# RMSNorm with every row written twice: the first load of each group in two transfers of 512 rows, gamma in two DMAs

## The chip, the cores and the metric

The kernel runs on one core of one Trainium2 chip. The metric is the device time of one launch in microseconds (us); lower is better. The time before is the median of three runs, 238.38 us (238.24 to 238.87). A profile is one more execution of the same program, recorded by the hardware profiler: its own time was 238.07 us, of which 236.2 us lie between the first and the last instruction of the core (the span). All times of the trace count from the start of that span.

The core's engines run their own instruction streams side by side: ACT (the scalar engine), DVE (the vector engine), POOL and SP. SP does no arithmetic here; it issues the DMAs of x and of the output. A DMA runs on 16 DMA engines, which cut it into packets.

## The reference

```python
def reference(x, gamma):          # x: (8, 512, 2048) float32, gamma: (2048,) float32
    B, S, D = x.shape
    x_rep = np.repeat(x, 2, axis=1)
    rms = np.sqrt((x_rep ** 2).mean(axis=-1, keepdims=True) + 1e-6)
    x_norm = x_rep / rms
    return (x_norm * gamma[None, None, :]).astype(np.float32)
```

Each of the 4096 rows of x (2048 floats, 8 KB) is divided by its root mean square, multiplied by gamma, and written twice, one copy right behind the other. So 33.55 MB are read and 67.11 MB written.

## The kernel before

**Tiles.** The rows are taken in four blocks of 1024 (index n). In a block, partition p holds eight neighbouring rows (H * K = 8), 64 KB of x in one piece: `x_t` at line 36 is the view. One DMA loads a block (8.39 MB). Its output has 2048 rows and is stored in two DMAs (h = 0, 1) of 8.39 MB each: for h, partition p writes the doubled copies of its rows 4h to 4h + 3, 64 KB in one piece, so neighbouring partitions lie 128 KB apart in the output (`out_t`, line 37). There are twelve such transfers in all, four loads and eight stores.

**Memory.** One buffer `y` (line 46) has 24 slots of one row (8 KB) a partition. `first` is slots 0 to 7, `second` 8 to 15, `third` 16 to 23; each is the size of one store. A group of two blocks is worked through by `four(n, ...)` (line 89), which is called for n = 0 and n = 2:

- block n is loaded into slots 4 to 11, that is the upper half of `first` and the lower half of `second`;
- block n + 1 is loaded into `third`;
- rows 0 to 3 of block n (slots 4 to 7) are scaled into the even slots of `first`, copied into the odd ones, and stored (h = 0);
- rows 4 to 7 of block n (slots 8 to 11) are scaled within `second`, from the last row to the first, copied and stored (h = 1);
- rows 0 to 3 of block n + 1 go from `third` into `first`, which has to wait until the first store has read `first`; then rows 4 to 7 are spread within `third`. Both are copied and stored.

**Instructions.** `squares` (line 57) takes the sum of squares of one row a partition on ACT (line 63) and then the root of all rows of the call (line 67). `scale` (line 70) has a reciprocal on DVE (line 73) and one multiplication by the row's factor and by gamma (line 75). `repeat` (line 80) makes the second copies, on ACT or on DVE (line 82).

**Order.** The schedule is written by hand: each engine works its instructions in the order in which the program lists them, and the framework adds the waits that the slots need. On SP the order in a group is load n, load n + 1, then the four stores; SP waits at each one until its slots may be read or written, and what stands behind it waits too. In the second group the load of block 2 (slots 4 to 11) has to wait for the second and the third store of the first group, the load of block 3 for the fourth.

**Gamma.** `constants` (line 121) loads gamma on ACT's queue into partition 0 of `y`, as a staging place: 16 pieces of 125 floats in one DMA (line 122), and three DMAs of 16 floats (line 128). POOL then spreads it over all partitions into `gamma_b` in two broadcasts (lines 132 and 136). The same function sets the epsilon and has ACT load its table with a first root (line 140).

Of the kernel before, what the change touches and what calls it, by code (L numbers as in the profile page):

```python
# [1 line left out]

# [4 lines left out]


@with_exitstack
def kernel(  # L10
    ctx: ExitStack,
    tc: tile.TileContext,
    x: bass.AP,
    gamma: bass.AP,
    out: bass.AP,
):
    nc = tc.nc
    P = nc.NUM_PARTITIONS
    f32 = mybir.dt.float32
    Act = mybir.ActivationFunctionType  # L20
    Alu = mybir.AluOpType

    B, S, D = x.shape
    Bo, So, Do = out.shape
    R = So // S
    assert R == 2 and D == Do and B == Bo and So == S * R
    eps = 1e-6
    inv_d = 1.0 / float(D)


    K = 4
    N = B * S
    ntiles = N // (P * K)
    assert N % (P * K) == 0 and ntiles == 8
    H = 2
    x_t = x.rearrange("b s d -> (b s) d").rearrange("(n p k) d -> n p k d", p=P, k=H * K)
    out_t = out.rearrange("b s d -> (b s) d").rearrange("(n p h j) d -> n h p (j d)", p=P, h=H, j=K * R)

    singles = ctx.enter_context(tc.tile_pool(name="singles", bufs=1))
    rows = ctx.enter_context(tc.tile_pool(name="rows", bufs=1))  # L40
    junk = ctx.enter_context(tc.tile_pool(name="junk", bufs=1, space=bass.MemoryType.PSUM))
    small = ctx.enter_context(tc.tile_pool(name="small", bufs=4))

    y = rows.tile([P, 3 * K * R, D], f32, name="y")
    first, second, third = 0, K * R, 2 * K * R

    def load(n, at):
        nc.sync.dma_start(out=y[:, at : at + H * K, :], in_=x_t[n])  # L50

    def store(n, h, to):
        nc.sync.dma_start(
            out=out_t[n, h], in_=y[:, to : to + K * R, :].rearrange("p j d -> p (j d)")
        )

    def squares(at, rows):

        n = len(rows)
        ss = small.tile([P, n], f32, name=f"ss{n}")  # L60
        for c, k in enumerate(rows):
            sq = junk.tile([P, D], f32, name="sq")
            nc.scalar.activation(  # L63
                out=sq[:], in_=y[:, at + k, :], func=Act.Square, accum_out=ss[:, c : c + 1]
            )
        rms = small.tile([P, n], f32, name=f"rms{n}")
        nc.scalar.activation(out=rms[:], in_=ss[:], func=Act.Sqrt, scale=inv_d, bias=eps_t[:])  # L67
        return rms

    def scale(at, to, rows, rms):  # L70
        n = len(rows)
        rstd = small.tile([P, n], f32, name=f"rstd{n}")
        nc.vector.reciprocal(out=rstd[:], in_=rms[:])  # L73
        for c, k in enumerate(rows):
            nc.vector.scalar_tensor_tensor(  # L75
                out=y[:, to + R * k, :], in0=y[:, at + k, :], scalar=rstd[:, c : c + 1],
                in1=gamma_b[:], op0=Alu.mult, op1=Alu.mult,
            )

    def repeat(to, k0, k1, copy):  # L80
        y_r = y[:, to + R * k0 : to + R * k1, :].rearrange("p (k r) d -> p k r d", r=R)
        copy(out=y_r[:, :, 1, :], in_=y_r[:, :, 0, :])  # L82

    ctx.enter_context(tc.manual_schedule())

    half = K // 2
    up, down = list(range(K)), list(range(K - 1, -1, -1))

    def four(n, constants, step):


        load(n, first + K)
        constants()
        load(n + 1, third)
        for rows in (up[:half], up[half:]):
            scale(first + K, first, rows, squares(first + K, rows))
        repeat(first, 0, half, nc.scalar.copy)
        repeat(first, half, K, nc.vector.tensor_copy)
        store(n, 0, first)
        scale(second, second, down, squares(second, down))  # L100
        repeat(second, half, K, nc.scalar.copy)
        for k in range(0, half, step):
            repeat(second, k, k + step, nc.vector.tensor_copy)
        store(n, 1, second)
        roots = [squares(third + h * K, up) for h in range(H)]
        scale(third, first, up, roots[0])
        repeat(first, 0, half, nc.scalar.copy)
        repeat(first, half, K, nc.scalar.copy)
        store(n + 1, 0, first)
        scale(third + K, third, up, roots[1])  # L110
        repeat(third, 0, K, nc.scalar.copy)
        store(n + 1, 1, third)

    gamma_b = singles.tile([P, D], f32, name="gamma_b")
    G, E = 16, 3
    C = D // G - E
    gamma_s = y[0:1, 0:2, :].rearrange("p k (c d) -> p (k c) d", c=G // 2)
    gamma_t = y[0:1, 2, :]
    eps_t = singles.tile([P, 1], f32, name="eps_t")

    def constants():
        nc.scalar.dma_start(
            out=gamma_s[0:1, :, :C],
            in_=gamma[: G * C].rearrange("(p c d) -> p c d", p=1, c=G),
        )
        for c in range(E):
            at = G * C + c * G
            nc.scalar.dma_start(
                out=gamma_t[0:1, c * G : (c + 1) * G],
                in_=gamma[at : at + G].partition_broadcast(1),  # L130
            )
        nc.gpsimd.partition_broadcast(  # L132
            out_ap=gamma_b[:, : G * C].rearrange("p (c d) -> p c d", c=G),
            in_ap=gamma_s[0:1, :, :C],
        )
        nc.gpsimd.partition_broadcast(out_ap=gamma_b[:, G * C :], in_ap=gamma_t[0:1, : E * G])  # L136
        nc.vector.memset(eps_t, eps)  # L137

        root = singles.tile([P, 1], f32, name="root")[:]
        nc.scalar.activation(out=root, in_=eps_t[:], func=Act.Sqrt)  # L140

    four(0, constants, half)
    four(2, lambda: None, 1)


# [1 line left out]
_INS = ['x', 'gamma']  # L147
_OUTS = [((8, 1024, 2048), 'float32')]


# [23 lines left out]
```

## Time and profile before

| what | value |
|---|---|
| median of three runs | 238.38 us (238.24 to 238.87) |
| time of the profiled execution | 238.07 us |
| its span | 236.2 us |
| L75 DVE, scaling of one row, x32 | 73.8 us, 2349 ns each |
| L63 ACT, squares of one row, x32 | 60.1 us, 1878 ns each |
| L82 ACT, copies, x10 | 42.6 us, 4283 ns each |
| L82 DVE, copies, x5 | 9.2 us, 1865 ns each |
| L132 and L136 POOL, broadcasts of gamma | 2243 and 323 ns |
| ACT's idle time before L63, ended by the load of x | 70.4 us, twice |

How to read it: a line number is that of the printed kernel. "Busy" is the sum of the durations of a group of instructions; the idle time before a group is put down to what ended it. The share of a DMA queue is the time that its packets took, out of the span of all 16 DMA engines. A release by a DMA is the moment when the transfer's last part has landed.

### The profile page before, as it was taken

Reading aid. Unit: us, or ns where it says so; the run is one execution under the profiler, and the core shown is the slowest. Engines: PE = TensorE matmul, PEld = TensorE weight load, DVE = VectorE, ACT = ScalarE, POOL = GpSimd, SP = SyncE. Lnnn points to the kernel's source line nnn. Section 1 sums busy time; section 2 is a strip of 40 time slices with the busy share of each in tenths; the row PEclk is TensorE's granted clock in tenths of the full one; section 3 lists DMA queues with packets and bytes.
Section 4 is the critical chain, followed back from the end, with each engine's and each line's share of the span. In section 5 each row is a group of like instructions: output and inputs, shape, how many; then the busy total and the mean of one; then the engine's idle time right before and its main releaser. Section 6 shows DMA issues by size and latency. Waiting matters only on the chain.

```text
span 236.2 us, 226 instructions
## 1 busy us (share of the span) xinstructions
DVE 84.5 (36%) x48; ACT 110.2 (47%) x86; POOL 2.8 (1%) x6
## 2 busy tenths in 40 slices
DVE  0000396594699500000000007928919992000000
ACT  2001989479998470000000049991999957400000
POOL 0110000000000000000000000000000000000000
DMA  9898989989898989989898998989898998989894
GB/s 355 356 533 355 510 377 422 466 366 522 355 533 356 533 355 422 466 377 510 355 533 355 488 400 355 533 355 533 355 533 355 488 399 355 533 355 533 355 533 178
DMA packets 1767, 100.68 MB, mean 426 GB/s; under 512 B 230, under 2 KB 230, under 8 KB 230
## 3 DMA queue, kind: packets, MB, share of 16 engines
q1 hardware_dynamic: 1728, 100.66, 98.7%
q10 hardware_dynamic: 38, 0.01, 0.0%
q14 instruction: 1, 0.01, 0.0%
HBM read 33.56 MB, written 67.11 MB: 426 GB/s over the span
## 4 chain that ended last, share of the span: by engine, by line
DMA 45%; ACT 26%; DVE 12%; issue 2%; DVEq 0%
DMA y<-in_x_dram 26%; DMA out_dram<-y 20%; ACT sq L63 15%; DVE y L75 12%; ACT y L82 11%; ACT rms L67 1%; DVE rstd L73 0%; DVEq L75 0%
## 5 line engine op out<-in xcount | busy, mean ns | idle before, releaser
L63 ACT ACTIVATE sq<-y 128x2048 f32<-128x2048 f32 x32 | 60.1, 1878 | 71.1 <-DMA y<-in_x_dram 70.4
L75 DVE SCALAR_TENSOR_TENSOR y<-y,rstd,gamma_b 128x2048 f32<-128x2048 f32 x32 | 73.8, 2349 | 1.6 <-DMA out_dram<-y 1.0
L82 ACT COPY y<-y 128x4096 f32<-128x4096 f32 (+1 forms) x10 | 42.6, 4283 | 19.1 <-DVE y L75 18.3
L73 DVE RECIPROCAL rstd<-rms 128x4 f32<-128x4 f32 (+1 forms) x10 | 1.7, 170 | 109.2 <-ACT rms L67 109.2
L82 DVE COPY y<-y 128x4096 f32<-128x4096 f32 (+1 forms) x5 | 9.2, 1865 | 0.1
L63 ACT ACTIVATION_READ_ACCUMULATOR sq<-y 128x1 f32 x32 | 6.0, 186 | 0.0
L67 ACT ACTIVATE rms<-ss,eps_t 128x4 f32<-128x4 f32 (+1 forms) x10 | 3.0, 297 | 0.3
L140 ACT ACT_TABLE_LOAD x1 | 1.3, 1283 | 2.6 <-issue 2.6
L132 POOL PARTITION_BROADCAST gamma_b<-y x1 | 2.2, 2243 | 10.2 <-DMA y<-in_gamma_dram 10.2
L136 POOL PARTITION_BROADCAST gamma_b<-y x1 | 0.3, 323 | 10.1 <-DMA y<-in_gamma_dram 10.1
L137 DVE MEMSET eps_t<- 128x1 f32 x1 | 0.1, 59 | 0.8 <-PEq L158 0.8
L140 ACT ACTIVATE root<-eps_t 128x1 f32<-128x1 f32 x1 | 0.2, 203 | 0.0
L158 POOL MEMSET const-bfloat16-1.0<- 128x1 bf16 x1 | 0.1, 102 | 0.0
L158 POOL MEMSET const-float32-0.0<- 128x1 f32 x1 | 0.1, 99 | 0.2 <-issue 0.2
L158 POOL MEMSET const-uint8-127<- 128x1 uint8 x1 | 0.1, 101 | 0.0
L158 POOL MEMSET const-float32-1.0<- 128x1 f32 x1 | 0.1, 98 | 0.0
## 6 DMA issues: line engine op xcount, KB each, us to landing
out_dram<-y SPq DMA_DIRECT2D x8, 24.8
y<-in_x_dram SPq DMA_DIRECT2D x4, 31.4
y<-in_gamma_dram ACTq DMA_DIRECT2D x3, 0.1 KB
y<-in_gamma_dram ACTq DMA_DIRECT2D x1, 7.8 KB, 9.8
```

What stands on the lines that cost most here:

```text
L63: nc.scalar.activation(out=sq[:], in_=y[:, at + k, :], func=Act.Square, accum_out=ss[:, c : c + 1])
L67: nc.scalar.activation(out=rms[:], in_=ss[:], func=Act.Sqrt, scale=inv_d, bias=eps_t[:])
L73: nc.vector.reciprocal(out=rstd[:], in_=rms[:])
L75: nc.vector.scalar_tensor_tensor(out=y[:, to + R * k, :], in0=y[:, at + k, :], scalar=rstd[:, c : c + 1], in1=gamma_b[:], op0=Alu.mult, op ...
L82: copy(out=y_r[:, :, 1, :], in_=y_r[:, :, 0, :])
L132: nc.gpsimd.partition_broadcast(out_ap=gamma_b[:, : G * C].rearrange("p (c d) -> p c d", c=G), in_ap=gamma_s[0:1, :, :C],)
L136: nc.gpsimd.partition_broadcast(out_ap=gamma_b[:, G * C :], in_ap=gamma_t[0:1, : E * G])
L137: nc.vector.memset(eps_t, eps)
L140: nc.scalar.activation(out=root, in_=eps_t[:], func=Act.Sqrt)
L158: nc = _bacc.Bacc("TRN2", target_bir_lowering=False, num_devices=1)
```

## The change

The blocks with an even n (0 and 2, the first of each group) are laid out in another way. Such a block of 1024 rows is taken as two halves of 512 rows. In a half, partition p holds four neighbouring rows (32 KB of x). The load is two DMAs of 4.19 MB each: half 0 into slots 4 to 7, half 1 into slots 8 to 11. The stores of the block follow: store h writes the doubled rows of half h, again 64 KB a partition in one piece, with neighbouring partitions 64 KB apart. Blocks 1 and 3 are loaded and stored as before.

Gamma is now loaded straight into partition 0 of `gamma_b`, in two DMAs on ACT's queue, each of 16 pieces of 64 floats (w = 2048 / 16 / 2 = 64), and spread by one broadcast that reads row 0 of `gamma_b` and writes all of it.

```diff
-    x_t = x.rearrange("b s d -> (b s) d").rearrange("(n p k) d -> n p k d", p=P, k=H * K)
-    out_t = out.rearrange("b s d -> (b s) d").rearrange("(n p h j) d -> n h p (j d)", p=P, h=H, j=K * R)
+    x_r = x.rearrange("b s d -> (b s) d").rearrange("(n m) d -> n m d", m=P * H * K)
+    out_r = out.rearrange("b s d -> (b s) d").rearrange("(n m) d -> n m d", m=P * H * K * R)
+
+    def apart(n):
+        return n % 2 == 0
+
+    def x_t(n):
+        if apart(n):
+            return [x_r[n].rearrange("(h p k) d -> h p k d", h=H, p=P)[h] for h in range(H)]
+        return [x_r[n].rearrange("(p k) d -> p k d", p=P)]
+
+    def out_t(n, h):
+        if apart(n):
+            return out_r[n].rearrange("(h p j) d -> h p (j d)", h=H, p=P)[h]
+        return out_r[n].rearrange("(p h j) d -> h p (j d)", p=P, h=H)[h]
...
     def load(n, at):
-        nc.sync.dma_start(out=y[:, at : at + H * K, :], in_=x_t[n])
+        views = x_t(n)
+        w = H * K // len(views)
+        for h, rows in enumerate(views):
+            nc.sync.dma_start(out=y[:, at + h * w : at + (h + 1) * w, :], in_=rows)
 
     def store(n, h, to):
         nc.sync.dma_start(
-            out=out_t[n, h], in_=y[:, to : to + K * R, :].rearrange("p j d -> p (j d)")
+            out=out_t(n, h), in_=y[:, to : to + K * R, :].rearrange("p j d -> p (j d)")
         )
...
-    G, E = 16, 3
-    C = D // G - E
-    gamma_s = y[0:1, 0:2, :].rearrange("p k (c d) -> p (k c) d", c=G // 2)
-    gamma_t = y[0:1, 2, :]
     eps_t = singles.tile([P, 1], f32, name="eps_t")
 
     def constants():
-        nc.scalar.dma_start(
-            out=gamma_s[0:1, :, :C],
-            in_=gamma[: G * C].rearrange("(p c d) -> p c d", p=1, c=G),
-        )
-        for c in range(E):
-            at = G * C + c * G
-            nc.scalar.dma_start(
-                out=gamma_t[0:1, c * G : (c + 1) * G],
-                in_=gamma[at : at + G].partition_broadcast(1),
-            )
-        nc.gpsimd.partition_broadcast(
-            out_ap=gamma_b[:, : G * C].rearrange("p (c d) -> p c d", c=G),
-            in_ap=gamma_s[0:1, :, :C],
-        )
-        nc.gpsimd.partition_broadcast(out_ap=gamma_b[:, G * C :], in_ap=gamma_t[0:1, : E * G])
+        G, E = 16, 2
+        w = D // G // E
+        g_in = gamma.rearrange("(p c d) -> p c d", p=1, c=G)
+        g_to = gamma_b[0:1, :].rearrange("p (c d) -> p c d", c=G)
+        for c in range(0, D // G, w):
+            nc.scalar.dma_start(out=g_to[:, :, c : c + w], in_=g_in[:, :, c : c + w])
+        nc.gpsimd.partition_broadcast(out_ap=gamma_b[:], in_ap=gamma_b[0:1, :])
```

## The prediction

> **What bounds the kernel now.** I read the head of the page first, then the queue part, then a table of stretches, then the chain of waits with the issue times of the SP queue. The page says at once that no compute engine is the bound:
>
> ```profile
> span 236.2 us, 226 instructions
> DVE 84.5 (36%) x48; ACT 110.2 (47%) x86; POOL 2.8 (1%) x6
> ...
> q1 hardware_dynamic: 1728, 100.66, 98.7%
> q10 hardware_dynamic: 38, 0.01, 0.0%
> ...
> HBM read 33.56 MB, written 67.11 MB: 426 GB/s over the span
> ```
>
> ACT works less than half of the span and DVE a third, while the packets of the SP queue (q1) take 98.7% of what 16 DMA engines have. 33.56 MB must be read and 67.11 MB written, and the change alters neither. A mean can hide a stage with another limit, so I cut the span at the times at which each of the twelve 8.39 MB transfers has its first packet (from the packet records of the trace: load 0, load 1, four stores, load 2, load 3, four stores). The columns are the stretch and its length, busy time of each engine, the clock, the DMA share and GB/s:
>
> ```profile
> 1.73:21.64 19.91, 0.00 (x0) 1.49 (x2) 2.24 (x1) 1.00 1.01 422
> 21.64:41.00 19.36, 11.85 (x7) 17.40 (x16) 0.32 (x1) 1.00 1.00 433
> 41.00:60.32 19.32, 11.70 (x6) 14.26 (x14) 0.00 (x0) 1.00 1.00 434
> ...
> 98.95:118.69 19.74, 0.00 (x0) 0.00 (x0) 0.00 (x0) 1.00 0.99 425
> 118.69:138.01 19.32, 0.00 (x0) 0.00 (x0) 0.00 (x0) 1.00 1.00 434
> 138.01:157.33 19.32, 11.85 (x7) 17.66 (x16) 0.00 (x0) 1.00 1.00 434
> 157.33:176.65 19.32, 11.77 (x7) 14.23 (x15) 0.00 (x0) 1.00 1.00 434
> ...
> 215.29:235.00 19.71, 0.00 (x0) 0.00 (x0) 0.00 (x0) 1.00 0.98 426
> ```
>
> Every stretch has a DMA share of about 1.00, whether compute runs beside it or not, and lasts 19.32 us, for loads and stores alike. The records give the unit: a packet is one partition's 65,536 bytes and takes 2.418 us; 8 packets an engine and one semaphore write of 9 ns make 19.35. So 96 x 2.418 = 232.13 us of 236.2 are data, 12 x 0.009 = 0.11 semaphores. The last stretch is cut at its end (235.0), so its 19.71 holds the drain of the engine that started 0.4 us late and is no loss. What is left of idle time inside the stream is 0.59 us in the first stretch (the first packet of each engine took 2.8 to 3.5 us) and 0.42 in the sixth. Before the stream lie 1.73 us, after it 1.23.
>
> The chain of waits names compute lines, which misleads here:
>
> ```profile
> 0.72 21.92 DMA y<-in_x_dram
> ...
> 76.17 23.86 DMA out_dram<-y
> ...
> 100.04 38.78 DMA y<-in_x_dram
> ...
> 155.30 22.23 DMA out_dram<-y
> ```
>
> A "DMA" piece lasts from issue to landing, so it holds time in which the transfer queues behind another. The load issued at 100.04 lands 38.78 us later because 19 of these belong to the store ahead of it. The compute pieces between them are work done while older transfers drain. What decides is whether each transfer is issued before the previous one runs dry: the first store is issued at 39.20 and has its first packet at 41.00 (1.80 ahead), the next at 55.89 for 60.32, 76.17 for 79.64, 87.08 for 98.95; in the second group 155.30 for 157.33 (2.03 ahead), 172.02 for 176.65, 192.23 for 195.97. An issue needs about 1.0 us to its first packet (0.72 to 1.73 at the start). No store is late; the thinnest cover is 1.80 - 1.01 = 0.79 us.
>
> **The change part by part.**
>
> *Loads 0 and 2 in two halves, compute sooner.* The first half is 4.19 MB, so it lands 4 x 2.418 = 9.67 us sooner: the squares of line 63 start at 22.65 - 9.67 = about 13.0 instead of 22.67, and the first store is issued at 39.20 - 9.67 = 29.5. It then waits in the ring behind load 1 until 41.1. The second store goes out at 46.2 instead of 55.89, still ahead of 60.4. The third store cannot move as far, since its scaling writes the slots that the first store reads, and that store lands at 61.48 (the DVE wait on out_dram there); it gains about 2 us of cover, from 76.17 to some 74.2, because the squares of the third block are done sooner and only DVE then holds back the copies of line 82. In the second group load 2 still waits for the third store (100.04), load 3 for the fourth (119.74); the halves land near 129.1 and 138.9, and the store of 155.30 goes out near 145.6. All of this is cover. The stream had none to fill, so its worth is 0.0 us.
>
> *Moved waits.* The second half's issue stands behind the first on SP; its slots 8 to 11 were read by the second store, done near 81, so it adds no wait. Behind it on SP are load 1 (at the start) and load 3, each put back by one issue of 0.34 to 0.42 us: load 1 goes out near 1.6 and its first packet isn't due before 21.6; load 3 waits for the fourth store's landing anyway, 18 us ahead of its own first packet. POOL's queue has the broadcast alone. If the cover were gone, each issue would cost its 0.34 us; it is 11 us and more.
>
> *More packets.* Here lies the only cost. A partition's part of a half load is 32,768 bytes, so loads 0 and 2 take 256 packets instead of 128 each: 8 more an engine and load, 16 in all. No x packet of that size is in the trace, so I bound it. The packet records give 9 ns for 4 bytes, 11 for 64, 26 for 500 and 2418 for 65,536. A line through the last two has a slope of 2392 / 65,036 = 0.03678 ns a byte and starts at 26 - 18.4 = 7.6 ns; the 8 KB packets of instruction fetch (queue 14) at 307 to 309 lie on it (301 + 7.6). A 32 KB packet is then 1,213 ns, and 16 more packets cost 16 x 7.6 = 0.12 us. Lower bound: 0, as no size beats the slope. Upper bound: the dearest 8 KB fetch took 512 ns, 211 above its bytes, so 16 x 0.204 more = 3.3 us over the 0.12. I take 0.12, because the fetches beside a full stream and four sizes lie on one line, while the 512 is from before the span, on an idle chip.
>
> *The address pattern.* Neighbouring partitions of those loads now lie 32 KB apart, of their stores 64 KB apart instead of 128. The two spacings in the trace (64 KB loads, 128 KB stores) both give 2418 ns, so I take 0; below nothing there is no room at 1.00 share. As an upper end I use the dearest x packet of the early stretch past the first ones, 2506 (3.6% over): 38.6 us of such loads would cost 1.4 us.
>
> *Two more transfers.* One semaphore packet of 9 ns an engine each: 0.02 us. The stretches show that nothing else lies between two transfers of a queue (19.36 and 19.32 against 19.35).
>
> The Trainium skill, "DMA: Bandwidth & Descriptors", section "Anatomy of one DMA — SWDGE (gpsimd) path", speaks against this: it fits a fixed cost of about 2.0 us, mostly the wait for the write's receipt, to every DMA issued from GpSimd. By that fit in series the two added transfers would cost 4.0 us, an estimate that ends at 242.4. This trace's back-to-back stretches disagree for queued transfers, and the measurement decides.
>
> *Gamma.* Before: 26 + 9 ns on each engine, and three 64-byte pieces with semaphores (3 x 20 ns) on one. After: two pieces of 256 bytes (by the line 17 ns each) and two semaphores, 52 ns on every engine. Between -0.04 and +0.02 us. When gamma comes matters more: in the trace a gamma packet gets its turn after each x packet; its first stands behind two x packets, at 7.1. With shorter x packets that is 5.0 (counted in packets) to 7.1 (in time), and three more turns of 1.21 us end at 8.6 to 10.8. One broadcast of 2,048 columns (2.24 x 2048 / 2000 = 2.3 us, against 2.24 + 0.32) is done by 11 to 13.2. DVE needs gamma_b at 27.34 - 9.67 = 17.7, so it is hidden by 4 us, and behind that by the 11 us of the first store. The ACT queue issues two DMAs instead of four before its table load, some 0.6 us less, all before 13.0.
>
> **Sum.** 238.07 (the profiled execution: 236.2 of span and 1.87 around it) + 0.12 + 0.02 + 0.0 = 238.2; the median of the runs shown lies 0.31 above that execution, so 238.38 + 0.14 = **238.5 us**.
>
> **Rivals.**
> *Slower: a price at each packet boundary.* Place: the 32 KB packets of loads 0 and 2. A measurement of this kernel can tell about 0.3%, 0.72 us, from no change. That is reached at 0.72 / 16 = 45 ns an extra packet, six times the 7.6; the 512 ns fetch would make it 241.8. The address pattern would need loads 1.9% slower, and its end is 239.9. For it: neither is in the trace. Against it: the line through four sizes, and the equal rates at two spacings.
> *Faster: the compute chain sets the end.* The waits list ACT 70.4 us idle for x, and the whole head start of 9.67 would give 228.7. Against: 232.13 us of packets and 2.96 at the ends are a floor of 235.1 in the span, 237.0 in time. All the same, 0.59 us of slow first packets could halve with their size (-0.3) and the 0.42 in the sixth stretch may not come back: 237.8.
> *The change doesn't start compute sooner,* since packets of both halves may be served in turn and land together. For: queues are served in turn. Against: both halves are in one ring, and load 1 landed 19.4 us after load 0, in order. It would end at 238.5 too, as nothing waits for the compute.
>
> **Chances.** Forecast and its idle twin: 80% within 0.3%. Slower by a packet or address price: 14%. Faster: 6%. The forecast's own range is 238.2 to 238.9, the spread of the runs around it; I reach down to 237.8 (the two idle pieces won back) and up to 239.4, where some of the slower rival is held and its far end, under 1 in 10, is left out.
>
> **What would show it.** Right: q1 with 128 x 2 more data packets plus 32 semaphores (2016), each 32 KB packet near 1.213 us; load stretches of 19.4 to 19.5; first squares near 13.0, first store issued near 29.5 with its first packet still near 41.1; third store's landing near 100. Wrong: 32 KB packets over 1.26 us, a stretch with a DMA share under 0.95 anywhere past 22 us, or a first packet before 1.5 us or later than 2.

## The result, and the profile after

The changed kernel takes 239.63 us (median of six runs, 239.1 to 240.0) against 238.39 us (238.24 to 238.87) before: a ratio of 1.0049 with a 95% interval of 1.0033 to 1.0065. It is 1.24 us slower, where +0.14 was forecast. The profiled execution took 240.0 us.

The head of the page after, and its queue part:

```profile
span 238.1 us, 221 instructions
DVE 84.5 (35%) x48; ACT 110.8 (47%) x86; POOL 2.5 (1%) x5
...
q1 hardware_dynamic: 2016, 100.66, 98.4%
q10 hardware_dynamic: 64, 0.01, 0.0%
```

2016 packets on q1 are the forecast count, and the 512 packets of 32 KB took a median of 1.213 us, the forecast price. Busy times hardly moved. The chain of waits after (start, length, what) shows that the compute at the start did what was forecast:

```profile
0.72 12.21 DMA y<-in_x_dram
...
12.96 2.01 ACT sq L79 x2
...
17.62 4.63 DVE y L91 x2
...
29.49 33.00 DMA out_dram<-y
```

Half 0 lands at 12.9, the squares start at 12.96 (forecast 13.0), and the first store is issued at 29.49 (29.5). So the loss isn't late compute. The table of stretches after, cut at the first packet of each transfer as before (stretch and length, DVE, ACT, POOL, clock, DMA share, GB/s), shows where it is:

```profile
1.75:21.58 19.83, 4.13 (x3) 9.98 (x12) 2.29 (x1) 1.00 0.99 418
21.58:42.14 20.56, 15.55 (x10) 14.85 (x11) 0.00 (x0) 1.00 1.00 408
42.14:61.46 19.32, 4.05 (x3) 17.07 (x19) 0.00 (x0) 1.00 1.00 434
...
100.10:119.41 19.31, 0.00 (x0) 0.00 (x0) 0.00 (x0) 1.00 1.00 434
119.41:138.78 19.37, 4.20 (x3) 8.49 (x10) 0.00 (x0) 1.00 1.00 433
138.78:158.10 19.32, 14.31 (x9) 13.68 (x11) 0.00 (x0) 1.00 1.01 435
...
216.05:236.97 20.92, 0.00 (x0) 0.00 (x0) 0.00 (x0) 1.00 0.93 401
```

Three things changed. Load 1, a whole load that the diff doesn't touch, lasts 20.56 us instead of 19.36. The fourth store is back at 19.31, where it took 19.74 before. And the last stretch is 20.92 long instead of 19.71 because the 16 engines no longer end together: their last packets end 1.6 us apart, 0.39 before. DMA share is 1.00 even in the long stretch of load 1: the engines aren't idle, their packets last longer. The packet records name them: the last packet of load 1 on each of the 16 engines, begun between 38.5 and 39.2, took 3.2 to 4.3 us instead of 2.418, 1.19 us over on the mean. What queues directly behind these packets is the first store, issued at 29.49, some 12 us ahead of its turn; before, it was issued at 39.20, while the last packets were already under way.

### The profile page after: what moved, and what is told of

Read it like the earlier page. It is cut to its first block, busy times and chain, and to the rows that moved or that the text cites. A ratio compares the mean times of both kernels' runs of the same rounds, so it can differ in the third digit from the quotient of the medians.

```text
span 238.1 us, 221 instructions
## 1 busy us (share of the span) xinstructions
DVE 84.5 (35%) x48; ACT 110.8 (47%) x86; POOL 2.5 (1%) x5
## 3 DMA queue, kind: packets, MB, share of 16 engines
q1 hardware_dynamic: 2016, 100.66, 98.4%
## 4 chain that ended last, share of the span: by engine, by line
DMA 56%; DVE 15%; ACT 14%; issue 1%; DVEq 0%; SPq 0%
DMA out_dram<-y 38%; DMA y<-in_x_dram 17%; DVE y L91 15%; ACT y L98 7%; ACT sq L79 6%; ACT rms L83 0%; DVE rstd L89 0%; DVEq L91 0%; SPq L66 0%
## 5 line engine op out<-in xcount | busy, mean ns | idle before, releaser
L140 POOL PARTITION_BROADCAST gamma_b<-gamma_b x1 | 2.3, 2294 | 10.2 <-DMA gamma_b<-in_gamma_dram 10.2
```

The costliest lines, as they stand in the source:

```text
L140: nc.gpsimd.partition_broadcast(out_ap=gamma_b[:], in_ap=gamma_b[0:1, :])
```

## The experiments

All 18 were run beside the kernel before on the same chip. Ratios are to it (its median was 238.05 to 238.26 beside them), with 95% intervals. A "turn" is a change from loads to stores or back on the queue: the first is the one behind load 1.

**again**: the changed kernel unchanged, for a second profile.

> The changed kernel once more, for a second profile. Theory (the hand-over): the first store, queued 12 us ahead, holds up the last packets of load 1, so the same packets are slow again: 1 to 2 us lost between 38 and 43 us on all 16 engines, and the time is again 239.1 to 240.0. Rival (chance stall): the slow packets lie elsewhere or are gone, the time keeps within 0.3% of 239.6 all the same or falls to 238.5.

239.28 us, ratio 1.0041 (1.0027 to 1.0054). The stretches of load 1 and of the fourth store:

```profile
21.77:42.05 20.28, 15.28 (x10) 14.57 (x12) 0.00 (x0) 1.00 1.00 414
...
100.01:119.33 19.32, 0.00 (x0) 0.00 (x0) 0.00 (x0) 1.00 1.00 434
```

The same packets are slow on all 16 engines, by 1.02 us on the mean. It is no chance stall.

**late_store**: a 4-byte DMA on SP, which reads a scaled row of the second half of the same block, holds the first store back. (The expectation calls it a row of the next block; it is one of rows 4 to 7 of this one.)

```diff
+        scale(second, second, down, squares(second, down))
+        nc.sync.dma_start(out=gate[0:1, 0:1], in_=y[0:1, second + R * 2, 0:1])
         store(n, 0, first)
-        scale(second, second, down, squares(second, down))
...
+    gate = singles.tile([P, 1], f32, name="gate")
```

> Same halves and same early compute, but the first store of each group is issued only once a row of the next block is scaled (near 39.5 and 156 instead of 29.5 and 146.6). Theory (the hand-over): load 1 ends without slow packets, the stretch of load 1 is back at 19.3 us, the time falls to 238.4 to 238.7. Rival (compute beside the load, or packet size, or rows in another order): 239.3 to 240.0, slow packets near 38.5 still there.

**one_transfer**: new rows and 32 KB packets in a single DMA.

```diff
+        if apart(n):
+            nc.sync.dma_start(
+                out=y[:, at : at + H * K, :].rearrange("p (h k) d -> p h (k d)", h=H),
+                in_=x_r[n].rearrange("(h p k) d -> p h (k d)", h=H, p=P),
+            )
...
```

> Rows laid out as in the changed kernel and 32 KB packets, but one DMA for the whole block, so compute and first store come as late as before. Theory (the hand-over): 238.4 to 238.7, that is before plus the 0.12 us of more packets. Rival (packet size or rows in another order cost the time): 239.3 to 240.0.

**old_layout**: two DMAs, rows to partitions as before, for the stores too (the part not shown removes the new `out_t`).

```diff
...
-        views = x_t(n)
-        w = H * K // len(views)
+        w = K if apart(n) else H * K
+        eight = x_r[n].rearrange("(p k) d -> p k d", p=P)
+        views = [eight[:, c : c + w, :] for c in range(0, H * K, w)]
```

> Two DMAs of four rows a partition and early compute as in the changed kernel, but eight neighbouring rows stay with a partition and the stores lie 128 KB apart as before. Theory (the hand-over): as slow as the changed kernel, 239.1 to 240.0, slow packets at the end of load 1. Rival (rows in another order cost the time): 238.4 to 238.7.

late_store took 239.99 (1.006 to 1.0098): the slow packets near 38.5 are gone, yet the time is worse. one_transfer took 239.83 (1.0036 to 1.0079), three runs near 239.0 and four of 239.8 to 240.5; the profile is of one that took 238.97, and it has no slow packets of size at load 1 (0.06 us). old_layout took 239.39 (1.0032 to 1.0059) with 1.28 us at load 1. So the order of the rows isn't the cause, the slow packets at load 1 come with the early store, and without them the time is lost elsewhere. All of these kernels carry the new gamma, which made it the next suspect.

**hold**: the changed kernel, with one small ACT instruction ahead of the first squares that waits for the second half.

```diff
+        held = small.tile([P, 1], f32, name="held")
+        nc.scalar.activation(out=held[:], in_=y[:, first + K + H * K - 1, 0:1], func=Act.Square)
         for rows in (up[:half], up[half:]):
```

> The changed kernel in all but one thing: one small ACT instruction reads the last slot of the second half ahead of the first squares of a group, so compute and the first store start as late as before (first store near 39.2 and 156), with two load DMAs, 32 KB packets, the new rows and the new gamma kept. Theory (a first store queued long before load 1 ends holds up the last packets of load 1): no slow packets near 38.5, 238.3 to 238.8. Rival (the split loads or gamma cost the time themselves): slow packets elsewhere, 239.2 to 240.0.

**gamma_only**: the kernel before with the new `constants` alone.

> The kernel before with the new gamma alone. Theory: as before, 238.1 to 238.6, no slow packets at the end of load 1 and 0.2 to 0.4 us lost at the end of the fourth store, as the profile before has it. Rival (gamma's packets shift the 16 engines against each other and this sets the time): 239 or more.

**first_only** and **second_only**: the changed kernel with `return n == 0` or `return n == 2` in `apart`.

> The new layout and two loads for block 0 alone; block 2 is loaded and stored as before. Theory (first store queued early): the whole cost is in the first group, slow packets near 38.5 on all engines worth 1.0 to 1.3 us, 239.2 to 239.8. Rival (each split load costs its share): about half of it, 238.7 to 239.0.

> The new layout and two loads for block 2 alone, block 0 as before. Theory (it is the first turn from loads to stores that costs, not each): 238.2 to 238.8, slow packets at the end of load 3 of under 0.2 us. Rival (each turn with a store queued early costs 1.2 us and the first one merely came first): slow packets near 155 of 1 us or more, 239.2 to 240.0.

gamma_only is the surprise: 239.18, ratio 1.0045 (1.0033 to 1.0057), though its profile has no slow load 1. The first stretch is load 1, then the fourth store, load 2 and load 3:

```profile
21.67:41.00 19.33, 11.85 (x7) 17.35 (x16) 0.00 (x0) 1.00 1.00 434
...
99.00:118.57 19.57, 0.00 (x0) 0.00 (x0) 0.00 (x0) 1.00 1.00 429
118.57:137.93 19.36, 0.00 (x0) 0.00 (x0) 0.00 (x0) 1.00 1.00 433
137.93:157.31 19.38, 11.85 (x7) 17.47 (x16) 0.00 (x0) 1.00 1.01 433
```

Its span is 237.0, 0.75 over before, of which the engines' spread at the end is 0.69 (1.08 against 0.39); the other 0.36 lie outside the span (239.18 less 236.97, where the profile before has 238.07 less 236.23). hold took 239.79 (1.0049 to 1.0075), without slow packets at load 1, so the theory's 238.3 to 238.8 fell. first_only took 239.31 (1.004 to 1.0064), 0.90 us at load 1: the split of block 0 alone costs as much as both. second_only took 240.04 (1.0069 to 1.0105): with a late first store load 1 is clean, and now the last packets of load 3, ahead of the early store of the second group, are slow, by 0.68 us on the mean and 1.44 at most. That is nearer to the rival: the second turn isn't immune, it was cheap only where the first had been dear (0.07 and 0.03 us in the two profiles of the changed kernel).

**split_only**: the changed kernel with the old gamma (`constants` and its views as before).

> The two split loads, their layout and the early compute with the gamma of the kernel before (one DMA of 16 pieces and three DMAs that run on one DMA engine). Theory (the new gamma alone costs the time, the split only 0.14): 238.1 to 238.5. Rival (an early first store has its own price at the turn from loads to stores): 239 to 239.6 with slow packets near 38.5.

**gamma_four, gamma_one, gamma_spare**: the kernel before with gamma in four DMAs (E = 4), in one (E = 1), and in one beside three idle DMAs on one engine:

```diff
+        for c in range(3):
+            nc.scalar.dma_start(
+                out=spare[0:1, c * G : (c + 1) * G],
+                in_=gamma[c * G : (c + 1) * G].partition_broadcast(1),
+            )
```

> The kernel before, gamma in four DMAs of 16 pieces of 32 floats and one broadcast: as many DMAs in all as before (16), none on one engine alone. Theory (what counts is the packets that one engine alone has to carry): 238.9 to 239.5, as with two DMAs. Rival (the number of DMAs in the program counts): 238.0 to 238.3.

> The kernel before, gamma in one DMA of 16 pieces of 128 floats and one broadcast. Theory (one engine's extra packets are missing): 238.9 to 239.5. Rival (the two DMAs of small pieces were the price): 238.0 to 238.3.

> As gamma_one, and three DMAs of 16 floats each on one engine into a spare tile that nothing reads: the trickle of the kernel before without its use. Theory: 238.0 to 238.3, the trickle alone brings the time of before back. Rival (the place or the shape of the gamma load counts): 238.9 to 239.5.

split_only took 239.37 (1.0035 to 1.0061), with 0.97 us at load 1. The theory that gamma alone costs the time fell: either part alone costs about 1.1 to 1.2 us, and both together no more. gamma_one took 238.81 (1.0004 to 1.0038), gamma_spare 238.67 (1.0012 to 1.0029), gamma_four 239.94 (1.0057 to 1.0083). So three idle DMAs on one engine don't bring the time of before back, and the price goes up with the number of 16-piece DMAs: ratios of 1.0021, 1.0045 and 1.0070 for one, two (gamma_only) and four, though the intervals of one and two overlap a little.

**late_load**: the kernel before, load 2 delayed by ACT work into a slot that it overwrites.

```diff
+    def hold(n):
+        for w in [D] * 8 + [D // 2] if n else []:
+            nc.scalar.activation(out=y[:, first + K, :w], in_=gamma_b[:, :w], func=Act.Square)
...
+        hold(n)
         load(n, first + K)
```

> The kernel before; in the second group ACT first squares gamma nine times into a slot of block 2 that the load overwrites, from the landing of the third store (100) on, so that load 2 is issued near 116.5 instead of 100.04, some 2 us ahead of its turn. Theory (a transfer of the other direction that is queued long before the turn slows the last packets ahead of it): no slow packets near 116, the stretch of the fourth store 19.3 instead of 19.74 us, 237.6 to 237.9. Rival (the turn from stores to loads costs this much in any case): 238.0 to 238.5.

238.54, ratio 1.0013 (1.0004 to 1.0021): load 2 was issued at 116.78, and it didn't help. The third and fourth store, and load 2:

```profile
79.71:99.03 19.32, 0.39 (x1) 7.02 (x1) 0.00 (x0) 1.00 1.00 434
99.03:118.35 19.32, 0.00 (x0) 16.33 (x9) 0.00 (x0) 1.00 1.00 435
118.35:137.87 19.52, 0.00 (x0) 0.00 (x0) 0.00 (x0) 1.00 1.01 430
```

The fourth store is clean, as the theory has it, but the loss moved behind the turn, into the first packets of load 2. The rival holds here: the turn from stores to loads costs its few tenths whether the load is queued early or late.

**gamma_pad, before_pad, after_pad**: 20 more tiny ACT instructions at the start of gamma_only, of the kernel before and of the changed kernel.

```diff
         nc.scalar.activation(out=root, in_=eps_t[:], func=Act.Sqrt)
+        for _ in range(20):
+            nc.scalar.activation(out=root, in_=eps_t[:], func=Act.Sqrt)
```

> The kernel before with the new gamma alone (239.18), and 20 more tiny ACT instructions of 0.2 us at the start, while ACT waits for x. Theory (with fewer instructions the 8 KB instruction fetch falls at 152.5, in load 3 just before a turn, and its engine, held back, sets the end; more instructions move it to the stores near 70): 238.0 to 238.5. Rival (the gamma packets themselves cost the time): 238.9 to 239.5 with the fetch near 70.

> The kernel before with the same 20 ACT instructions; the fetch of 75 moves to an earlier place. Theory: a place that is not just before a turn changes nothing (238.0 to 238.6); should it fall between 30 and 41, ahead of the turn to stores, 238.6 to 240. Rival: 238.0 to 238.6 wherever it falls.

> The changed kernel with the same 20 ACT instructions. Theory: the fetch leaves load 3 (144), so the spread of the 16 engines at the end shrinks from 1.0 to 1.6 us to under 0.9, while the 1 to 1.2 us of slow packets at the end of load 1 stay: 238.9 to 239.3. Rival (only the early store counts): 239.2 to 240.0 as without them.

They move the one 8 KB instruction fetch inside the span, which takes one of the 16 engines 0.31 us: from 152.5 to 53.3, from 75.0 to 43.8 and from 144.2 to 44.8. gamma_pad took 238.71 (1.0012 to 1.0042), between the two forecasts, but with single runs at 239.85 and 240.39; the first of these is the profiled one, and there one engine lost 0.7 us near 156 without any fetch. So the place of the fetch may be part of gamma's price and isn't all of it: inconclusive. before_pad is the same as before (238.23, 0.9994 to 1.0011). after_pad took 239.25 (1.0026 to 1.0053), 0.96 us at load 1: the time fits both forecasts, and the spread of 1.02 is not under 0.9, as the theory had it, nor much changed, so it decides nothing.

**split_hold**: split_only with hold's ACT instruction, that is the split with the old gamma and a late first store.

> The two split loads and their layout, the gamma of the kernel before, and ACT held until the second half of the load has landed, so that the first store is issued near 39.4 instead of 29.5. Theory (it is the early first store that makes the split cost 1.2 us): no slow packets at the end of load 1, 238.2 to 238.7. Rival (two load DMAs of 32 KB packets have a price of their own, at the turn to load 2 too): 239.0 to 239.8 without slow packets at load 1.

**early_store**: the kernel before, with an early first store and no split. It leaves out the squares and roots of rows 0 to 3 of block 0 (their factor is 1), so that their scaling needn't wait for ACT; the part not shown adds ten of the tiny ACT instructions of before_pad, and with them the instruction fetch stays near its place (71.3 for 75.0).

```diff
+    def ones():
+        rms = small.tile([P, half], f32, name="ones")
+        nc.vector.memset(rms, 1.0)
+        return rms
...
-            scale(first + K, first, rows, squares(first + K, rows))
+            scale(first + K, first, rows, squares(first + K, rows) if n else ones())
...
```

> The kernel before, gamma and whole loads as they were; the squares and roots of rows 0 to 3 of block 0 are left out (the factor is 1 there), and 10 tiny ACT instructions keep the instruction fetch in its place. DVE then starts at 23.4 and the first store is issued near 35.1 instead of 39.2, 6 us ahead of its turn. Theory (an early first store alone slows the last packets of load 1): slow packets near 38.6 on most engines, 0.7 to 1.2 us, the loss at the end of the fourth store gone, 238.5 to 239.3. Rival (the split is needed for it): 238.0 to 238.4, none near 38.6.

early_store settles the main question: 239.28, ratio 1.0042 (1.003 to 1.0054). Whole loads, the old gamma, and a first store issued 3.7 us sooner, in the timelines of the SP queue before and here:

```profile
39.20 0.35 SPq L53 DMA_DIRECT2D out_dram<-y  x1
35.52 0.35 SPq L53 DMA_DIRECT2D out_dram<-y  x1
```

and in its table of stretches load 1, the first store, the fourth store and load 2:

```profile
21.68:42.06 20.38, 13.64 (x9) 11.81 (x10) 0.32 (x1) 1.00 1.00 412
42.06:61.38 19.32, 10.03 (x6) 16.15 (x15) 0.00 (x0) 1.00 1.00 434
100.02:119.34 19.32, 0.00 (x0) 0.00 (x0) 0.00 (x0) 1.00 1.00 434
119.34:138.65 19.31, 0.00 (x0) 0.00 (x0) 0.00 (x0) 1.00 1.00 434
```

That is the signature of the changed kernel, made by an earlier issue: load 1 a microsecond longer, the fourth store 0.42 shorter. The compute beside load 1 isn't the cause: DVE and ACT work 13.64 and 11.81 us of it here, 11.85 and 17.40 before, and in both kernels all 112 packets of load 1 ahead of the last 16 took 2.42 to 2.43 us. split_hold, the counterpart, shows that the split isn't free either once its store is late, as its rival had it: 239.78 (1.0038 to 1.0082), one run at 238.37 and five at 239.7 to 240.2. Its stretches of load 1, the fourth store and the two halves of load 2:

```profile
21.82:41.14 19.32, 11.85 (x7) 17.46 (x17) 0.00 (x0) 1.00 1.00 434
99.16:118.82 19.66, 0.00 (x0) 0.00 (x0) 0.00 (x0) 1.00 1.02 428
118.82:138.41 19.59, 0.00 (x0) 0.00 (x0) 0.00 (x0) 1.00 0.98 420
```

Load 1 is clean, and the price is now paid at the turn to load 2: 0.34 us in the fourth store and 0.23 in load 2 on the first engine (19.59 against 19.36, where two halves are undisturbed), and more on the slowest, so that the spread of the engines is 1.30 us at the end. On the engine that ends last, the fourth store and load 2 together take 1.47 us more than before; in hold it is 1.86, in late_store 1.49. So that is where the three kernels with a split and a late first store lose most of their time.

Worked out from the packet records of every profile: the mean excess of the last packet of load 1 over 2.418 us, the length of the fourth store (first engine to first engine), and how far apart the 16 engines end; beside the median time. A profile is of one execution: that of gamma_pad took 239.85, of one_transfer 238.97, of second_only 240.65, the others came within 0.4 us of their medians.

```
kernel        first store  load 1's last  fourth   spread   median
              issued       packet, over   store    at end   time
before        39.20        0.01           19.74    0.39     238.39
before_pad    39.34        0.01           19.58    0.59     238.23
late_load     39.28        0.01           19.32    0.81     238.54
gamma_spare   39.16        0.09           19.59    0.69     238.67
gamma_pad     39.12        0.06           19.57    1.81     238.71
gamma_one     39.01        0.02           19.55    0.55     238.81
gamma_only    39.30        0.02           19.58    1.08     239.18
split_hold    39.37        0.00           19.66    1.30     239.78
hold          39.41        0.00           19.77    1.32     239.79
one_transfer  39.15        0.06           19.71    0.70     239.83
gamma_four    39.41        0.07           19.55    2.47     239.94
late_store    40.12        0.00           19.88    0.85     239.99
second_only   39.28        0.00           19.62    2.18     240.04
after_pad     29.76        0.96           19.32    1.02     239.25
early_store   35.52        1.06           19.32    0.77     239.28
again         29.86        1.02           19.32    0.97     239.28
first_only    29.72        0.90           19.32    0.98     239.31
split_only    29.63        0.97           19.32    0.79     239.37
old_layout    29.70        1.28           19.32    0.77     239.39
after         29.49        1.19           19.32    1.59     239.63
```

All seven profiles (of six kernels) with a first store issued before 36 have 0.9 to 1.3 us at the end of load 1 and none at the fourth store; all thirteen with one at 39 or later have under 0.1 there and, late_load apart, 0.2 to 0.6 at the fourth store.

## Why the prediction was wrong, point by point

**The bound was right.** The stream of packets is the limit: every stretch keeps a DMA share near 1.00 but the last (0.93, as the engines end apart), and no stretch of the changed kernel waits for a compute engine. Two of the prediction's own signs went against it: that share under 0.95, and the first store's first packet at 42.14 instead of near 41.1.

**The terms that were costed were right, all but gamma's.** Packets: 1.213 us each as forecast, and load 2 lasts 19.37 us instead of 19.32 where 0.07 more was forecast. Load 0 can't show its share, since its end scatters by more from kernel to kernel (21.58 to 21.83 in two halves, 21.60 to 21.79 whole). Head start, gamma's arrival (broadcast from 10.65 to 12.94, forecast done by 11 to 13.2), second store (46.11, forecast 46.2): all as worked out. The third store went out at 75.42, not 74.2, and no time hung on it. One premise was thinner than it reads: of the instruction fetches only one ran beside the full stream (309 ns); the one of 307 was, like that of 512, from before the span.

**The step that failed** is the one on the early compute: "All of this is cover. The stream had none to fill, so its worth is 0.0 us." A first store issued early isn't only cover. It made the last packets of the load ahead of it slower on all 16 engines, by 1.19 us on the mean in the profile after. early_store shows the same (1.06) with none of the change's edits in it, and costs 1.1 us. This is how the changed kernel loses its time; but taking the early store away doesn't bring the time back (hold, split_hold), since the turn to load 2 then costs as much or more. So a second step failed too: of the added packets the prediction says "Here lies the only cost", and a split with a late store costs 1.6 us (split_hold) where 0.14 was forecast. I took a transfer that waits in the ring to be free, from transfers that wait there behind others of the same direction (the third and fourth store are queued 3 and 12 us ahead, at no cost). Before, the only transfers queued far ahead of a turn were load 2, behind the fourth store, and the price of that turn stood in the trace: the 0.42 us of the sixth stretch, which I read as an idle piece that might not come back. late_load puts it at the turn, ahead of it or behind it.

**The sum, by the execution of again** (239.28, 1.21 over the profiled one before): load 0 +0.12, load 1 +0.93 (20.28 against 19.35 from first engine to first engine), fourth store -0.42, load 2 +0.04, spread of the engines at the end +0.58 (0.97 against 0.39), the ends of the span and what lies around it -0.04. In the profiled execution after, load 1 is +1.20 and the spread +1.20; that is 240.0. Followed on the engine that ends last, which is the one that counts, the lag behind the profile before grows in load 1 by 1.18 us in again and 1.22 after; the fourth store gives 0.13 back, and load 3 adds 0.02 in again and 0.88 after.

**The spread** was no term of mine at all: I read the 0.39 us by which the engines end apart before as "no loss". An engine that has fallen behind doesn't catch up: in the profile after the 16 engines end load 3 1.592 us apart, and each of the four stores behind it 1.591 or 1.592 apart. (In hold the spread falls from 1.97 to 1.32 there, but only because the engines ahead had to wait for a store issued at 157.31, 0.40 us before the first of them was through with load 3.) The slow packets at a turn aren't equally slow (0.8 to 1.9 us), an instruction fetch hits one engine alone, and the slowest sets the end.

**Gamma** was put between -0.04 and +0.02 by its packets. Alone it costs 1.1 us (gamma_only), 0.36 of it outside the span and most of the rest in the spread. The changed kernel doesn't have the 0.36 (1.88 outside the span against 1.84 before), and with the old gamma the split is no faster. So gamma's price is real by itself and isn't what makes the changed kernel slower; why it doesn't add up with the split's is open.

**The rivals.** The one that came true in sign, a price at each packet boundary, was wrong in its place: the median 32 KB packet took 1.213 us in every kernel that has them, and the slow ones are nearly all the first of load 0, which were slow at 64 KB too, and, in the kernels with a split and a late first store, those right behind the turn to load 2. The piece of the faster rival, the 0.42 us that "may not come back", did not come back, and was outweighed. The Trainium skill, "DMA: Bandwidth & Descriptors", section "Two DMAs through the same engine are not ordered", says that within one queue of one engine descriptors start in order but are pipelined, and that the engine's read and write sides are separate queues; a store behind a load could by that start its reads while the load still writes. No run here shows the two sides apart, so this is a reading and not a finding.

**Left open**: by what mechanism the queued store slows the load's last packets; why the later turns are cheap after a dear first one; why the split with a late store pays so much at the turn to load 2, and why split_hold takes 238.4 in one run of six and 239.7 or more in the others; and why one, two and four gamma DMAs cost more and more. No version that I ran is faster than the kernel before.

## What to carry to other kernels

In a kernel whose transfers run back to back, issuing a store sooner isn't free cover: where the queue turns from loads to stores, cut the stream at each transfer's first packet and compare the stretches on both sides of the turn, and treat a change of the issue time there as a change of the stream. Look at the slowest of the 16 DMA engines, not at their mean, since an engine that lost time keeps its lag to the end. And when a kernel stands 1.4 us above its floor (the prediction's 237.0), test each part of a change alone: here two parts cost 1.1 to 1.2 us each and 1.24 together.

## What the runs showed of the hardware that was not expected

The first turn from loads to stores slowed the last packet of the load by 0.9 to 1.3 us on the mean of the 16 engines when the store had been issued 6 to 12 us ahead, and by under 0.1 us when it was issued 1 to 2 us ahead, with the same bytes (early_store and before). At the second such turn an early store cost 0.68 us where the first had been cheap (second_only) and under 0.1 us where the first had been dear, so the lead alone doesn't decide it. A turn from stores to loads lengthened the fourth store by 0.2 to 0.6 us on the first engine in twelve kernels whose first turn had been cheap (late_load paid 0.2 in load 2), and by nothing in the seven profiles whose first turn had been dear. The time around the span isn't fixed: 1.8 and 1.9 us in the kernel before and in the changed one (238.07 less 236.23, 240.0 less 238.12), 1.6 to 2.0 us in most others, 2.2 us in gamma_only, gamma_one, gamma_spare, gamma_pad, one_transfer and second_only (239.18 less 236.97 in the first).
